# Instance normalisation on one core: the last tile stored in two pieces, and the final waits in the order of the stores

## The chip, the cores and the metric

The kernel runs on one core of a Trainium2 chip. The metric is the device time of one execution in microseconds (us). A profile shows the span from the first to the last instruction, some 1.7 us less than the device time. Even so, about one run in five of these kernels lies 1.5 to 7 us above the rest, so I quote medians, and for differences of a microsecond I read the profiles, where one event can be measured from another.

## The reference

```python
def setup_inputs():
    x = np.random.randn(8, 64, 32, 64, 64).astype(np.float32)   # 268 MB
    eps = np.float32(1e-5)

def reference(x, eps):
    mean = np.mean(x, axis=(2, 3, 4), keepdims=True)
    var = np.var(x, axis=(2, 3, 4), keepdims=True)
    return ((x - mean) / np.sqrt(var + eps)).astype(np.float32)
```

Each of the 512 instances (batch times channel) has 131072 elements. All of x is read once and written once.

## The kernel before

A tile has 128 rows (partitions) of 12288 floats: 6 MiB, three chunks of 4096 columns. There are 42 tiles in four buffers ("slots"), after two small parts of 2 MiB each. SyncE issues the loads, ScalarE the stores. VectorE and ScalarE share the work on a tile: sums, squares, and at the end the scaling, in place. VectorE scales chunks 0 and 1, ScalarE scales chunk 2, and then ScalarE issues the store:

```python
    # VectorE, end of a tile
        eng.reciprocal(out=a[:, SCALES : SCALES + 3], ...)._wait_ge(rooted[lane], c1)...
        eng.tensor_mul(out=a[:, SHIFTS : SHIFTS + 3], ...)...then_inc(shifted[lane], 1)
        eng.tensor_scalar(out=chunk[0], ...)._wait_ge(scaled[lane], c1).then_inc(done[lane], 1)
        eng.tensor_scalar(out=chunk[1], ...)._wait_ge(shifted[lane], c1).then_inc(done[lane], 1)

    # ScalarE, end of a tile
        eng.activation(out=chunk[2], ...)._wait_ge(shifted[lane], c1).then_inc(done[lane], 1)
        eng.dma_start(out=dst, in_=t)._wait_ge(done[lane], c3).then_inc(stored[lane], 16)

    # SyncE: loads
        ...
            eng.dma_start(out=slots[s][:], in_=x_t[it * SLOTS + s])._wait_ge(
                stored[s], c16).then_inc(landed[s], 16)
        ...
        for s in range(SLOTS):                       # the final waits
            eng.wait_ge(stored[s], 16 * len(range(s, n_tiles, SLOTS)))
```

The last tile is number 41, in slot 1, so its wait is the second of the four.

Of the kernel before, what the change touches and what calls it, by code (L numbers as in the profile page):

```python
# [9 lines left out]
def kernel(  # L10
# [20 lines left out]
    CHUNK = 4096  # L31
    THIRDS = 3
    COLS = THIRDS * CHUNK
    SLOTS = 4
    PART = P * CHUNK // n_elem

    n_tiles = n_inst // PART // THIRDS
# [7 lines left out]
    def tiles_of(ap):  # L45
        first = n_parts * P * CHUNK
        return ap[first : first + n_tiles * P * COLS].rearrange(
            "(k p f) -> k p f", p=P, f=COLS
        )

    def part_of(ap, m):
        return ap[m * P * CHUNK : (m + 1) * P * CHUNK].rearrange("(p f) -> p f", p=P)

    x_t, out_t = tiles_of(x_f), tiles_of(out_f)
# [24 lines left out]
    def semaphores(name, n=LANES):  # L79
        return [ctx.enter_context(nc.semaphore(f"{name}{i}")) for i in range(n)]  # L80
# [11 lines left out]
    done = semaphores("done")  # L92
    stored = semaphores("stored")
# [15 lines left out]
    def column(a, first, j):  # L109
        return a[:, first + j : first + j + 1]  # L110
# [95 lines left out]
            op1=Alu.add,  # L206
        )._wait_ge(shifted[lane], c1).then_inc(done[lane], 1)

    def tile_on_scalar(eng, t, lane, c1, c3, c4, c16, dst):
        a = small[lane]  # L210
        chunk = [t[:, i * CHUNK : (i + 1) * CHUNK] for i in range(THIRDS)]
        for j, part in ((1, chunk[1]), (2, chunk[2][:, : CHUNK - TURN])):
            eng.activation(  # L213
                out=unused[j - 1][:, : part.shape[1]],
                in_=part,
                func=Act.Identity,
                accum_out=column(a, SUMS, j),
            )._wait_ge(landed[lane], c16).then_inc(summed[lane], 1)
        for j in (1, 2):
            eng.activation(  # L220
                out=unused[j - 1][:],
                in_=chunk[j],
                func=Act.Square,
                bias=column(a, MEANS, j),
                accum_out=column(a, SQUARES, j),
            )._wait_ge(centred[lane], c1).then_inc(squared[lane], 1)
        eng.activation(  # L227
            out=a[:, ROOTS : ROOTS + 3],
            in_=a[:, VARS : VARS + 3],
            func=Act.Sqrt,  # L230
            bias=eps_t[:, 0:1],
        )._wait_ge(gathered[lane], c1).then_inc(rooted[lane], 1)
        eng.activation(  # L233
            out=chunk[2],
            in_=chunk[2],
            func=Act.Identity,
            scale=column(a, SCALES, 2),
            bias=column(a, SHIFTS, 2),
        )._wait_ge(shifted[lane], c1).then_inc(done[lane], 1)
        eng.dma_start(out=dst, in_=t)._wait_ge(done[lane], c3).then_inc(  # L240
            stored[lane], 16
        )

# [80 lines left out]
    def over_tiles(eng, on_part, on_tile, with_target=False):  # L324
        for m, (lane, t) in enumerate(parts):
            more = (part_of(out_f, m),) if with_target else ()
            on_part(eng, t, lane, *more)
        counts = [
            ctx.enter_context(eng.register(f"{on_tile.__name__}_c{m}"))
            for m in (1, 3, 4, 16)  # L330
        ]
        for c, m in zip(counts, (1, 3, 4, 16)):
            eng.reg_mov(c, m)
        with eng.Fori(0, ROUNDS) as it:
            for s in range(SLOTS):
                more = (out_t[it * SLOTS + s],) if with_target else ()
                on_tile(eng, slots[s][:], s, *counts, *more)
            for c, m in zip(counts, (1, 3, 4, 16)):
                eng.reg_add(c, c, m)
        for k in range(ROUNDS * SLOTS, n_tiles):  # L340
            c = k // SLOTS + 1
            more = (out_t[k],) if with_target else ()
            on_tile(eng, slots[k % SLOTS][:], k % SLOTS, c, 3 * c, 4 * c, 16 * c, *more)

    def load_all(eng):
        for m, (lane, t) in enumerate(parts):
            eng.dma_start(out=t, in_=part_of(x_f, m)).then_inc(landed[lane], 16)
        for s in range(SLOTS):
            load = eng.dma_start(out=slots[s][:], in_=x_t[s])
            if s >= SLOTS - n_parts:  # L350
                load._wait_ge(stored[s + n_parts], 16)
            load.then_inc(landed[s], 16)
        c16 = ctx.enter_context(eng.register("load_c16"))
        eng.reg_mov(c16, 16)
        with eng.Fori(1, ROUNDS) as it:  # L355
            for s in range(SLOTS):
                eng.dma_start(out=slots[s][:], in_=x_t[it * SLOTS + s])._wait_ge(  # L357
                    stored[s], c16
                ).then_inc(landed[s], 16)
            eng.reg_add(c16, c16, 16)  # L360
        for k in range(ROUNDS * SLOTS, n_tiles):
            eng.dma_start(out=slots[k % SLOTS][:], in_=x_t[k])._wait_ge(
                stored[k % SLOTS], 16 * (k // SLOTS)
            ).then_inc(landed[k % SLOTS], 16)

        for s in range(SLOTS):
            eng.wait_ge(stored[s], 16 * len(range(s, n_tiles, SLOTS)))

    def set_up(eng):
        count = 0  # L370
# [55 lines left out]
        return count  # L426

    load_all(nc.sync)
    set_by = set_up(nc.gpsimd)
    nc.vector.wait_ge(ready, set_by)  # L430
    over_tiles(nc.vector, part_on_vector, tile_on_vector)
    nc.tensor.wait_ge(ready, set_by)
    over_tiles(nc.tensor, part_on_tensor, tile_on_tensor)
    nc.scalar.preload_act_table(Act.Sqrt)
    nc.scalar.wait_ge(ready, set_by)
    over_tiles(nc.scalar, part_on_scalar, tile_on_scalar, with_target=True)


# [33 lines left out]
```

## Time and profile before

| | before |
|---|---|
| median of the first three runs | 1247.06 us (1246.88 to 1249.86) |
| span in the profile | 1245.2 us, granted clock 1.000 |
| moved | 536.89 MB, 431 GB/s over the span |
| busy: VectorE, ScalarE, DMA | 65%, 61%, 99.7% |

The page's row of tenths shows who is busy when; here the DMA row is full. For a change at the end of the kernel only the end counts, and there the average says nothing. 16 DMA engines share each store, 8 rows of the tile each, one packet per row, and each engine adds a small packet for the semaphore when its rows are through (the store queue's 6336 packets are 128 + 16 for each of its 44 stores).

### The profile page before, as it was taken

The page shows a single profiled execution, that of the slowest core. Times are in us where ns is not written, and L with a number is a line of the kernel's source. Part 1 is how long each engine was busy: PE and PEld are TensorE (multiplying, and loading weights), DVE is VectorE, ACT ScalarE, POOL GpSimd, SP SyncE. Part 2 cuts the span into 40 slices and gives each one's busy share as a digit, 9 for nine tenths or more (in the row PEclk, how much of TensorE's full clock was granted, in tenths as well). Part 3 has the DMA queues.
Part 4 walks back from the last instruction along what each step waited for, and adds up shares of the span by engine and source line. Part 5 has one row for each costly group of instructions (what it writes and reads, how often), then busy time and mean ns, then how long its engine had stood idle before and what let it go on. Part 6 is the DMA issues. An engine that isn't in the chain of part 4 may idle for free.

```text
span 1245.2 us, 1950 instructions
## 1 busy us (share of the span) xinstructions
PE 52.7 (4%) x176; PEld 44.1 (4%) x176; DVE 811.6 (65%) x724; ACT 757.7 (61%) x433; POOL 2.7 (0%) x15
## 2 busy tenths in 40 slices
PE   0000000000000000000000000000000000000000
PEld 0000000000000000000000000000000000000000
DVE  2887666666666666666666666666666666666663
ACT  5876555566666665665556665666566555566653
POOL 0000000000000000000000000000000000000000
DMA  9999999999999999999999999999999999999998
GB/s 396 429 430 434 444 433 429 431 429 441 439 433 431 429 429 444 436 429 433 431 433 442 434 431 431 429 434 444 433 431 431 429 442 437 431 433 429 429 444 368
DMA packets 12674, 536.89 MB, mean 431 GB/s; under 512 B 1408, under 2 KB 1408, under 8 KB 1408
## 3 DMA queue, kind: packets, MB, share of 16 engines
q1 hardware_dynamic: 6336, 268.44, 49.9%
q10 hardware_dynamic: 6336, 268.44, 49.8%
q14 instruction: 2, 0.02, 0.0%
HBM read 268.44 MB, written 268.44 MB: 431 GB/s over the span
## 4 chain that ended last, share of the span: by engine, by line
another core or an unknown queue 82%; DMA 9%; DVE 3%; ACT 2%; SPq 1%; issue 1%; PE 0%; ACTq 0%
DMA slot<-in_x_dram 6%; DMA out_dram<-slot 4%; ACT unused L220 2%; SPq L357 1%; DVE small L157 1%; DVE slot L200 1%; DVE slot L193 1%; ACT unused L213 0%; PE psum L250 0%; DVE small L137 0%; DVE small L125 0%; DVE small L131 0%; DVE small L143 0%; SPq L355 0%
## 5 line engine op out<-in xcount | busy, mean ns | idle before, releaser
L213 ACT ACTIVATE unused<-slot 128x4096 uint8<-128x4096 f32 x84 | 249.3, 2968 | 310.5 <-DMA slot<-in_x_dram 308.1
L157 DVE TENSOR_REDUCE small<-slot 128x1 f32<-128x4096 f32 x84 | 255.3, 3081 | 279.6 <-DMA slot<-in_x_dram 279.6
L220 ACT ACTIVATE unused<-slot,small 128x4096 uint8<-128x4096 f32 x84 | 310.8, 3701 | 65.3 <-DVE small L143 65.3
L171 DVE CUSTOM_DVE_ANT_0 unused<-slot 128x4096 uint8<-128x4096 f32 x42 | 185.9, 4426 | 1.4
L233 ACT ACTIVATE slot<-slot,small 128x4096 f32<-128x4096 f32 x42 | 159.7, 3802 | 18.5 <-DVE small L188 18.5
L200 DVE TENSOR_SCALAR slot<-slot,small 128x4096 f32<-128x4096 f32 x42 | 101.1, 2408 | 0.0
L164 DVE TENSOR_SCALAR slot<-slot,small 128x4096 f32<-128x4096 f32 x42 | 98.8, 2353 | 1.5
L250 PE MATMUL psum<-small,avg 128*128 128x12 f32 (+1 forms) x168 | 50.4, 375 | 1144.3 <-DVE small L125 1144.3
L193 DVE TENSOR_SCALAR slot<-slot,small 128x4096 f32<-128x4096 f32 x42 | 98.6, 2347 | 0.0
L250 PEld LDWEIGHTS psum<-small,avg 128*128 128x128 f32 x168 | 42.1, 311 | 1152.5 <-DVE small L125 1152.5
L131 DVE TENSOR_REDUCE small<-psum 128x3 f32<-128x12 f32 x84 | 14.2, 169 | 58.0 <-PE psum L250 58.0
L227 ACT ACTIVATE small<-small,eps_t 128x3 f32<-128x3 f32 x42 | 12.6, 299 | 62.6 <-DVE small L143 62.6
L125 DVE TENSOR_TENSOR small<-small,belongs 128x12 f32<-128x12 f32 x84 | 14.3, 170 | 31.9 <-ACT unused L220 29.5
L185 DVE RECIPROCAL small<-small 128x3 f32<-128x3 f32 x42 | 7.4, 176 | 15.4 <-ACT small L227 15.4
L137 DVE TENSOR_TENSOR small<-small,belongs 128x9 f32<-128x9 f32 x84 | 14.3, 170 | 2.9
L220 ACT ACTIVATION_READ_ACCUMULATOR unused<-slot,small 128x1 f32 x84 | 15.7, 186 | 0.0
L213 ACT ACTIVATION_READ_ACCUMULATOR unused<-slot 128x1 f32 x84 | 15.6, 186 | 0.0
L143 DVE TENSOR_REDUCE small<-small 128x3 f32<-128x9 f32 x84 | 13.6, 162 | 2.9
L263 DVE TENSOR_REDUCE small<-slot 128x1 f32<-128x2048 f32 x2 | 4.6, 2282 | 8.9 <-DMA slot<-in_x_dram 8.9
L289 ACT ACTIVATE unused<-slot,small 128x4096 uint8<-128x4096 f32 x2 | 7.4, 3707 | 2.0 <-DVE small L266 2.0
L286 ACT ACTIVATE unused<-slot 128x2048 uint8<-128x2048 f32 x2 | 3.8, 1910 | 7.1 <-DMA slot<-in_x_dram 6.6
L188 DVE TENSOR_TENSOR small<-small 128x3 f32<-128x3 f32 x42 | 6.8, 162 | 1.4
(26 smaller groups left out, 21.1 us busy)
## 6 DMA issues: line engine op xcount, KB each, us to landing
slot<-in_x_dram SPq DMA_DIRECT2D x42, 6144.0 KB, 39.9
out_dram<-slot ACTq DMA_DIRECT2D x42, 6144.0 KB, 54.2
slot<-in_x_dram SPq DMA_DIRECT2D x2, 2048.0 KB, 10.0
out_dram<-slot ACTq DMA_DIRECT2D x2, 2048.0 KB, 27.7
```

What stands on the lines that cost most here:

```text
L125: eng.tensor_tensor(out=block(a, by_both, n, m), in0=spread(a, at, m), in1=belongs[:, :, :m], op=Alu.mult,)._wait_ge(*wait).then_inc(steps ...
L131: eng.tensor_reduce(out=a[:, by_instance : by_instance + n], in_=p.rearrange("p (n m) -> p n m", m=m), axis=AXIS, op=Alu.add,)._wait_ge(st ...
L137: eng.tensor_tensor(out=block(a, by_chunk, n, n), in0=spread(a, by_instance, n), in1=belongs[:, :, :n].rearrange("p i c -> p c i"), op=Alu ...
L157: eng.reduce_sum(out=column(a, SUMS, j), in_=part, axis=AXIS)._wait_ge(landed[lane], c16).then_inc(summed[lane], 1)
L164: eng.tensor_scalar(out=chunk[0], in0=chunk[0], scalar1=column(a, MEANS, 0), scalar2=None, op0=Alu.add,)._wait_ge(centred[lane], c1).then_ ...
L171: eng.tensor_tensor_reduce(out=unused[2][:], in0=chunk[0], in1=chunk[0], scale=1.0, scalar=0.0, op0=Alu.mult, op1=Alu.add, accum_out=colum ...
L193: eng.tensor_scalar(out=chunk[0], in0=chunk[0], scalar1=column(a, SCALES, 0), scalar2=None, op0=Alu.mult,)._wait_ge(scaled[lane], c1).then ...
L200: eng.tensor_scalar(out=chunk[1], in0=chunk[1], scalar1=column(a, SCALES, 1), scalar2=column(a, SHIFTS, 1), op0=Alu.mult, op1=Alu.add,)._w ...
L213: eng.activation(out=unused[j - 1][:, : part.shape[1]], in_=part, func=Act.Identity, accum_out=column(a, SUMS, j),)._wait_ge(landed[lane], ...
L220: eng.activation(out=unused[j - 1][:], in_=chunk[j], func=Act.Square, bias=column(a, MEANS, j), accum_out=column(a, SQUARES, j),)._wait_ge ...
L233: eng.activation(out=chunk[2], in_=chunk[2], func=Act.Identity, scale=column(a, SCALES, 2), bias=column(a, SHIFTS, 2),)._wait_ge(shifted[l ...
L250: eng.matmul(out=p[:, col : col + THIRDS * m], lhsT=avg[PART][:], rhs=a[:, at + m : at + m + THIRDS * m], start=True, stop=True,)._wait_ge ...
```

## The change

The intent: in front of the last store the DMA engines seem to stand still for 2 us. If chunk 0 goes out as soon as it is scaled, the gap is filled. The other part puts the wait for the last tile behind the three others; its target is 16 higher, since the last tile now has two stores.

```diff
-    def tile_on_scalar(eng, t, lane, c1, c3, c4, c16, dst):
+    def tile_on_scalar(eng, t, lane, c1, c3, c4, c16, dst, last=False):
 ...
+        at = 0
+        if last:
+            at = CHUNK
+            eng.dma_start(out=dst[:, :at], in_=chunk[0])._wait_ge(
+                done[lane], c3 - 2
+            ).then_inc(stored[lane], 16)
         eng.activation(out=chunk[2], ...)._wait_ge(shifted[lane], c1).then_inc(done[lane], 1)
-        eng.dma_start(out=dst, in_=t)._wait_ge(done[lane], c3).then_inc(
+        eng.dma_start(out=dst[:, at:], in_=t[:, at:])._wait_ge(done[lane], c3).then_inc(
             stored[lane], 16
         )
 ...
-        for s in range(SLOTS):
-            eng.wait_ge(stored[s], 16 * len(range(s, n_tiles, SLOTS)))
+        for k in range(n_tiles - SLOTS, n_tiles):
+            uses = k // SLOTS + 1 + (k == n_tiles - 1)
+            eng.wait_ge(stored[k % SLOTS], 16 * uses)
```

(The caller passes `last` for tile 41 alone.) ScalarE's stream now has the wait for chunk 0 ahead of its own scaling of chunk 2.

## The prediction

> **What bounds the kernel now.** I read three things in this order: the DMA row and the queues of the page, the stretches of the whole span, and then the last 25 us in ever narrower stretches, because the change touches nothing earlier than the last tile.
>
> The page, DMA row of the 40 slices and the queues:
>
> ```profile
> DMA  9999999999999999999999999999999999999998
> ...
> q1 hardware_dynamic: 6336, 268.44, 49.9%
> q10 hardware_dynamic: 6336, 268.44, 49.8%
> ```
>
> The row stands at 9 from the first slice to the last but one. Loads (q1) and stores (q10) together take 99.7% of the 16 DMA engines' time, while VectorE has 65% and ScalarE 61%. The kernel is bound by its DMA engines. The stretches view with the first and last tiles cut off says how tightly (columns: stretch, its length, busy time of PE, PEld, DVE, ACT and POOL, clock, DMA share, GB/s):
>
> ```profile
> 55.00:1215.00 1160.00, 48.56 (x162) 40.61 (x162) 770.99 (x687) 710.39 (x405) 0.00 (x0) 1.00 1.00 434
> ```
>
> So only the two ends of the kernel can hold anything to gain. A store of a tile is 128 rows of 49152 bytes, which are 8 packets on each of the 16 engines; in the packet records one such packet takes 1.815 us (median of all), so one engine moves 27.1 GB/s. All 536.87 MB at 16 times that is 1239.1 us, of the 1245.2 us of the span: 6.1 us are not transfer.
>
> The end, as the timeline has it:
>
> ```profile
> 1222.87 0.16 DVE L188 TENSOR_TENSOR small<-small 128x3 f32<-128x3 f32 x1
> 1222.95 2.35 DVE L193 TENSOR_SCALAR slot<-slot,small 128x4096 f32<-128x4096 f32 x1
> 1223.07 3.80 ACT L233 ACTIVATE slot<-slot,small 128x4096 f32<-128x4096 f32 x1 [0.44 <-DVE small L188]
> 1225.21 2.41 DVE L200 TENSOR_SCALAR slot<-slot,small 128x4096 f32<-128x4096 f32 x1
> 1227.65 0.35 ACTq L240 DMA_DIRECT2D out_dram<-slot  x1
> ```
>
> VectorE scales chunk 0 (to 1225.30) and chunk 1 (to 1227.62); ScalarE scales chunk 2 beside it (to 1226.87); then the store is issued. The view of that issuing line says when it lands: 16.2 us later, at 1243.9.
>
> ```profile
> DMA to landing us min/median/max: 16.2/16.2/16.2
> ```
>
> What do the DMA engines do meanwhile? Stretches of the end; packets count where they start, so a share over 1.00 is a batch that starts together:
>
> ```profile
> 1222.00:1226.45 4.45, 0.00 (x0) 0.00 (x0) 4.02 (x6) 3.68 (x2) 0.00 (x0) 1.00 0.84 364
> 1226.46:1228.45 1.99, 0.00 (x0) 0.00 (x0) 1.16 (x1) 0.41 (x1) 0.00 (x0) 1.00 0.12 49
> 1228.45:1228.93 0.48, 0.00 (x0) 0.00 (x0) 0.00 (x0) 0.00 (x0) 0.00 (x0) 1.00 3.62 1536
> 1228.93:1230.30 1.37, 0.00 (x0) 0.00 (x0) 0.00 (x0) 0.00 (x0) 0.00 (x0) 1.00 0.08 36
> 1230.30:1241.20 10.90, 0.00 (x0) 0.00 (x0) 0.00 (x0) 0.00 (x0) 0.00 (x0) 1.00 1.00 433
> ...
> 1241.60:1243.00 1.40, 0.00 (x0) 0.00 (x0) 0.00 (x0) 0.00 (x0) 0.00 (x0) 1.00 0.08 35
> ```
>
> There is a hole in front of the last store, from 1226.46 to 1228.45. It is what the change means to fill. But it isn't a hole in all engines. The DMA view of 1226.46 to 1228.45 and that of 1228.93 to 1230.3:
>
> ```profile
> DMA packets 14, 0.10 MB, mean 49 GB/s; under 512 B 12, under 2 KB 12, under 8 KB 12
> ...
> DMA packets 1, 0.05 MB, mean 36 GB/s; under 512 B 0, under 2 KB 0, under 8 KB 0
> ```
>
> In the hole two whole rows start: 12 of the 14 packets are the small ones that count the semaphore. They are the last rows of the store before, on two engines that lag the other 14 by about one row. In the packet records their rows end at 1228.70 and 1228.93, when the new store has been in the queue for half a microsecond; 14 engines start its first row at 1228.51 to 1228.66, the last engine at 1228.934, the instant it is done with the old one. That engine (packets bear no engine here; I match each to the one that ended when it starts) then takes eight rows without a pause and ends at 1243.43, when the other 15 had ended at 1243.08 to 1243.24. **The engine that ends last had no hole.** The lag isn't a chance of this moment: between the first and the last of the 16 counts of a transfer lie 0.6 us at the first tile, 2.0 us a quarter of the way in and 2.2 to 2.6 us from the middle to the end, so it builds up and stays.
>
> **What the Trainium skill says.** "DMA: Bandwidth & Descriptors", section "Why a DMA increments its semaphore by 16 and not by 1": the engines of one transfer finish independently, and only the full count tells that all has landed. The trace agrees: of the store before the last, 14 counts came between 1226.79 and 1227.91, the two others at 1229.03 and 1229.42. The same page, "Anatomy of one DMA": waits are on the issuing sequencer, not in the DMA engines. It agrees too: the issue starts 0.03 us after VectorE ended; so a wait put in ScalarE's stream holds ScalarE. The same page, "Latency and other measured facts", has some 600 ns to the first byte for this kind of queue; here the first row starts 0.85 us after the issue starts and 0.50 us after it ends, and I use 0.85.
>
> **The change part by part.**
>
> First piece. ScalarE now waits for chunk 0 before it scales chunk 2. Chunk 0 is done at 1225.30 as before, the issue takes 0.35 us (1225.33 to 1225.68) and its rows can start at 1225.33 + 0.85 = 1226.18. The first engine is free at 1226.45, so 14 engines go straight on (from 1226.45 to 1227.56) and the two laggards at 1228.70 and 1228.93, as before. The hole closes: 14 engines gain between 1.0 and 2.1 us.
>
> ScalarE's part moves back. Chunk 2 starts at about 1225.73 in place of 1223.07, 2.66 us later, takes 3.80 us, and ends at 1229.53, after VectorE's chunk 1 (1227.62), so it now sets the second issue: 1229.55, 1.90 us later than the whole store was issued before. Its rows can start at 1229.55 + 0.85 = 1230.40.
>
> Is that late? Rows of 16384 bytes took 0.611 us (median of the early, small stores), so eight take 4.89 us. The earliest engine is through with the first piece at 1226.45 + 4.89 = 1231.34, 0.94 us after the second piece is there. ScalarE's delay is hidden.
>
> The last engine. Before: eight rows at 1.815 us, 14.52 us. From 0.611 us for 16384 bytes and 1.815 us for 49152, a row costs 0.009 us and 0.602 us per 16384 bytes, so one of 32768 is worth 1.213 us (an estimate). After: 8 x (0.611 + 1.213) = 14.59 us, and one semaphore packet more, 0.009 us: 0.08 us longer from the same start, 1228.93. It ends at about 1243.5. The other laggard ends at 1228.70 + 14.60 = 1243.3, the 14 at 1241.1 to 1242.2: they idle at the end in place of at the beginning.
>
> Final waits. Before, the last tile's wait comes second of four, and two that are long satisfied follow it; after, it is last. In the trace, the wait that ends with the landing ends at 1243.92, and one more waiting instruction lies at 1243.965 to 1244.00; the reordering is worth some 0.04 us.
>
> The sum: +0.08 - 0.04 = +0.04 us at the end, and nothing elsewhere, since loops and buffers are untouched. That is nothing.
>
> **The rivals.** (1) *The hole was on the path.* If all engines were alike, the store would end sooner by the 14 engines' gain, at most 1228.51 - 1226.45 = 2.06 us, and the slowest of them 1.0; 1245.0 to 1246.1 us. For it: the aggregate hole of 2 us is real, and the lag may be smaller in runs without a profile. (2) *The laggards speed up when the others are done*, because memory is less busy. Then part of the 1 to 2 us comes back. Against it: a laggard's row from 1226.88 to 1228.70 ran while 13 to 14 engines were idle and took 1.815 us, like all others. (3) *The later second piece takes the place of the hole*: if ScalarE or its issue took over 0.94 us longer than I reckon, the 14 engines would have a new gap; it would have to exceed some 2 us before they, and not the laggards, set the end. Time then 1247 to 1248. (4) *Short rows, 48 KiB apart, are slower in HBM* than rows that follow each other: 10% of 4.9 us would be 0.5 us. Nothing in this trace shows such rows.
>
> **Range and chances.** The base is 1247.06 us, the median of three (1246.88, 1247.06, 1249.86). With my sum it stays; rival 1, to which I give one in four, and rival 2, one in ten, draw it down by some 1.2 us, so I take off 0.3: 1246.8 us. Spread of runs (two within 0.2 us, the third 2.9 us above) is larger than any of these effects. Range 1245.3 to 1248.4. Two per cent are 25 us; the whole last store takes 16.2 us, so neither side can be reached by this change; 0.5% each for surprises.
>
> **What would show it right or wrong.** Right: two issues at about 1225.3 and 1229.55; ScalarE's last scaling starting near 1225.7; no hole in the DMA share at 1226.5 to 1228.5; in the last 2 us of transfer only one or two engines still busy; the landing at 1243.9 to 1244.0 and the span within 0.3 us. Wrong: a landing 1 us or more earlier (rival 1 or 2; the lag of the last engine tells which: gone, or rows shorter than 1.8 us per 48 KiB), a second hole at 1231 to 1232 (rival 3), or rows of the first piece over 0.65 us (rival 4).

## The result

| | before | changed |
|---|---|---|
| median, 6 runs of each | 1248.31 us (1246.72 to 1252.91) | 1247.05 us (1246.87 to 1247.35) |
| span in the profile | 1245.2 us | 1245.6 us |
| packets of the store queue | 6336 | 6480 |

The ratio is 0.9986, with a 95% interval from 0.9968 to 1.0004: the same. A ratio is the mean time of one kernel's runs over that of the other's of the same rounds, so not quite the ratio of the medians. It is the three high runs of before that pull it below 1; the lowest runs of the two are 0.15 us apart, the changed kernel's the higher.

The end of the changed kernel, as the timeline has it (start, length, engine, line, operation):

```profile
1223.32 2.35 DVE L193 TENSOR_SCALAR slot<-slot,small 128x4096 f32<-128x4096 f32 x1
1225.58 2.41 DVE L200 TENSOR_SCALAR slot<-slot,small 128x4096 f32<-128x4096 f32 x1
1225.70 0.35 ACTq L237 DMA_DIRECT2D out_dram<-slot  x1
1226.09 3.80 ACT L240 ACTIVATE slot<-slot,small 128x4096 f32<-128x4096 f32 x1 [3.10 <-DVE slot L193]
1229.92 0.34 ACTq L247 DMA_DIRECT2D out_dram<-slot  x1
```

Everything in this run is 0.37 us later than in the run before the change, because the last load landed that much later (1206.11 and 1205.74). Apart from that it is as reckoned: ScalarE stands idle for 3.10 us until VectorE has scaled chunk 0, issues the first piece, scales chunk 2, and issues the rest.

The stretches of the changed kernel (length, busy time of the five engines, clock, DMA share, GB/s; packets count where they start), and the packets of the first of them:

```profile
1226.53:1228.11 1.58, 0.00 (x0) 0.00 (x0) 1.46 (x1) 1.58 (x1) 0.00 (x0) 1.00 0.93 394
...
1231.49:1240.61 9.12, 0.00 (x0) 0.00 (x0) 0.00 (x0) 0.00 (x0) 0.00 (x0) 1.00 1.06 458
1240.61:1241.20 0.59, 0.00 (x0) 0.00 (x0) 0.00 (x0) 0.00 (x0) 0.00 (x0) 1.00 0.13 56
1241.42:1242.64 1.22, 0.00 (x0) 0.00 (x0) 0.00 (x0) 0.00 (x0) 0.00 (x0) 1.00 0.25 107
1242.64:1243.80 1.16, 0.00 (x0) 0.00 (x0) 0.00 (x0) 0.00 (x0) 0.00 (x0) 1.00 0.07 28
```

```profile
DMA packets 50, 0.62 MB, mean 394 GB/s; under 512 B 14, under 2 KB 14, under 8 KB 14
```

The hole is gone: where before the DMA share was 0.12 for 2 us, it is 0.93, and 36 rows start in 1.58 us. But the idle time has only moved. In the last 3 us the share falls to 0.25 and then 0.07, which is one engine of 16. In the packet records the engines end like this (the small packet for the semaphore included; a packet bears no engine number, so each is matched to the one that ended when it starts):

| | first 12 engines | next three | last engine |
|---|---|---|---|
| before | 1243.08 to 1243.20 | 1243.20 to 1243.24 | 1243.44 |
| changed | 1241.22 to 1241.83 | 1242.64 to 1242.84 | 1243.87 |

And the landings (the time from the start of an issue until the last of its 16 counts is in), from the views of the issuing lines: of tile 40's store, the first piece and the second piece.

```profile
DMA to landing us min/median/max: 30.9/30.9/30.9
...
DMA to landing us min/median/max: 9.0/9.0/9.0
...
DMA to landing us min/median/max: 14.4/14.4/14.4
```

So the last piece lands at 1229.92 + 14.4 = 1244.3, against 1243.9 before. Fifteen engines are done earlier, twelve of them by 1.4 to 1.9 us, and the kernel isn't.

### The profile page after: what moved, and what is told of

The parts are those of the page before. It is cut to its first block, busy times and chain, and to the rows that moved or that the text cites. A ratio compares the mean times of both kernels' runs of the same rounds, so it can differ in the third digit from the quotient of the medians.

```text
span 1245.6 us, 1951 instructions
## 1 busy us (share of the span) xinstructions
PE 52.6 (4%) x176; PEld 44.0 (4%) x176; DVE 811.4 (65%) x724; ACT 757.7 (61%) x433; POOL 2.7 (0%) x15
## 3 DMA queue, kind: packets, MB, share of 16 engines
q1 hardware_dynamic: 6336, 268.44, 49.9%
q10 hardware_dynamic: 6480, 268.44, 49.8%
## 4 chain that ended last, share of the span: by engine, by line
another core or an unknown queue 82%; DMA 9%; ACT 3%; DVE 2%; SPq 1%; issue 1%; PE 0%; ACTq 0%
DMA slot<-in_x_dram 6%; DMA out_dram<-slot 4%; ACT unused L221 2%; SPq L364 1%; DVE small L157 1%; DVE slot L193 1%; ACT unused L214 0%; DVE slot L200 0%; ACT slot L240 0%; PE psum L257 0%; DVE small L137 0%; DVE small L125 0%; DVE small L131 0%; DVE small L143 0%
## 6 DMA issues: line engine op xcount, KB each, us to landing
out_dram<-slot ACTq DMA_DIRECT2D x1, 4096.0 KB, 14.4
```

## The experiments

**Theory A:** the time is that of the DMA engine that lags, and this engine never had the hole: it was still writing the store before when the hole was open. **Theory B:** the hole was on the path and some of its gain was real, but was given back, by ScalarE's late start, by the second transfer or by the shorter rows. A minor question is whether the high runs of before have to do with the order of the waits.

Where two kernels or more were run together they ran on the same chip and share the runs of the kernel before.

### The changed kernel again

No edit.

> The changed kernel once more, beside the kernel before, for the spread of both. Theory A (the DMA engine that ends last never had the hole, so closing the hole is worth nothing): median 1246.9 to 1247.4, ratio to before 1.000 within 0.0005 among the runs without an outlier; in the profile the last engine again takes its rows of the last tile without a pause and is busy 1 us or more after most of the others. Theory B (the hole was on the path, and half of the gain shows): 0.999 or less, with the lowest runs 1 us below the lowest of before. Also open: the kernel before had three of six runs 2.7 to 6 us above its lowest, this one none; if that belongs to the kernels and not to chance, it comes again.

Measured: 1247.08 us median (1246.95 to 1253.76, 6 runs); before 1246.96 (1246.56 to 1252.16, 11 runs); ratio 1.0005, interval 0.9984 to 1.0026. In the profile 13 engines end at 1241.06 to 1241.67, two at 1242.59 and 1242.76, one at 1243.65. As theory A has it. The changed kernel has a high run too, 1253.76, so the high runs don't belong to the kernel before.

### The waits alone

```diff
-        for s in range(SLOTS):
-            eng.wait_ge(stored[s], 16 * len(range(s, n_tiles, SLOTS)))
+        for k in range(n_tiles - SLOTS, n_tiles):
+            eng.wait_ge(stored[k % SLOTS], 16 * (k // SLOTS + 1))
```

> The kernel before with only the final waits in the order of the stores; the last tile is stored whole. Theory A: no effect over 0.1 us on the span; the stretch from the last landing to the end of the span stays 1.28 to 1.31 us (1.28 before, 1.31 after the change). The step of the prediction (0.04 us gained) would make it 1.24. A theory that the order of the waits is what removes the slow runs of before expects no run here over 1248.5.

Measured: 1246.92 us (1246.70 to 1247.12, 6 runs), ratio 0.9993 (0.9979 to 1.0007), span 1245.2. From the last landing to the end of the span are 1.30 us, against 1.28 before: no gain. The trace shows why. The compiled program has its own order: in the changed kernel the wait for the last tile shares one instruction with that for tile 39 (it ends at 1244.386), and the wait for tile 38 still comes after it, on a branch at 1244.432. None of the six runs was high, but the next two kernels, which have this order of waits, have one each, so nothing follows from that.

### The first piece from another queue

The first piece is issued by SyncE; chunk 0's scaling counts a semaphore of its own (`early`), and ScalarE waits for nothing but the shift:

```diff
+        # SyncE, ahead of the final waits
+        eng.dma_start(out=out_t[k][:, :CHUNK], in_=slots[k % SLOTS][:, :CHUNK])._wait_ge(
+            early, 1).then_inc(stored[k % SLOTS], 16)
-        # ScalarE
-            eng.dma_start(out=dst[:, :at], in_=chunk[0])._wait_ge(done[lane], c3 - 2)...
```

> The first piece is issued from SyncE, which is idle then, and ScalarE no longer waits for VectorE before it scales chunk 2. So ScalarE ends 2.7 us sooner than in the changed kernel, and the second piece is issued 1.9 us sooner, when VectorE ends chunk 1. Theory A: nothing gained, landing and span as in the changed kernel within 0.5 us (the lag of the last engine differs from run to run by that), 1247.1. The rival that the gain of the hole was real and was given back by ScalarE's late start: 1 us or more faster, 1246.0 or less.

The timeline of this kernel:

```profile
1223.07 3.80 ACT L236 ACTIVATE slot<-slot,small 128x4096 f32<-128x4096 f32 x1 [0.44 <-DVE small L189]
1225.22 2.40 DVE L201 TENSOR_SCALAR slot<-slot,small 128x4096 f32<-128x4096 f32 x1
1225.33 0.34 SPq L374 DMA_DIRECT2D out_dram<-slot  x1
1227.65 0.35 ACTq L243 DMA_DIRECT2D out_dram<-slot  x1
```

Both pieces are in their queues as early as they can be, the second 1.9 us sooner than in the changed kernel, counted from the start of chunk 0's scaling (4.70 and 6.60 us). Measured: 1247.01 us (1246.81 to 1249.36), ratio 0.9997 (0.9982 to 1.0013), span 1245.3, last landing 1243.97. ScalarE's late start cost nothing; that form of theory B falls.

### The first piece late

```diff
-                done[lane], c3 - 2
+                done[lane], c3 - 1
```

> The changed kernel with the first piece held until VectorE has scaled chunk 1 too: both pieces later by 2.3 us (first issue as late as the whole store before, second issue 4.2 us after it). The hole of about 2 us is back in the engines that do not lag. Theory A: still 1247.1 and a landing within 0.5 us of the changed kernel's, because the last engine is free only 0.4 to 0.8 us after the first rows can start. Theory B, the hole on the path: 1 to 2 us slower than the changed kernel.

The stretches of this kernel and the landing of its second piece, which was issued at 1232.03:

```profile
1226.46:1228.65 2.19, 0.00 (x0) 0.00 (x0) 1.31 (x1) 0.45 (x1) 0.00 (x0) 1.00 0.11 45
1228.66:1230.00 1.34, 0.00 (x0) 0.00 (x0) 0.00 (x0) 1.34 (x1) 0.00 (x0) 1.00 1.31 550
```

```profile
DMA to landing us min/median/max: 12.1/12.1/12.1
```

The hole is back in full, 2.19 us at a share of 0.11, and the second piece is issued 2.3 us later than in the changed kernel, counted in the same way. It lands at 1244.1 all the same, and the median is 1246.90 us (1246.72 to 1250.36), ratio 0.9998 (0.9982 to 1.0015). With the hole the engines end together, 15 of them at 1243.33 to 1243.47 and one at 1243.64; without it they end apart, the last at the same time. This is the plainest evidence against theory B: the hole can be opened and closed and the time doesn't follow.

### The hole put on the path

If theory A holds, the same split has to pay as soon as all engines are idle and even when the last store comes. In both kernels VectorE waits, in the last tile only, until tile 40's store has landed:

```diff
+        if last:
+            k = n_tiles - 2
+            eng.wait_ge(stored[k % SLOTS], 16 * (k // SLOTS + 1))
         eng.reciprocal(out=a[:, SCALES : SCALES + 3], ...
```

> The kernel before, but VectorE waits, in the last tile alone and ahead of the reciprocal, until the store of the tile before has landed in full. So all 16 DMA engines are idle and even when the last store comes. About 6.8 us later than in the kernel before (landing of that store at 1229.4 in place of the reciprocal at 1222.66): scaling ends near 1234.4, first rows near 1235.3, landing near 1250.1, time near 1253.3. The engines should end within 0.2 us of each other.

> The same pause in the changed kernel. Theory A says that the split is worth nothing in the real kernel only because one engine is still behind; with all engines idle the first rows start 2.3 us sooner (VectorE's time for one chunk), the second piece is there 0.6 us before the first is through, and 0.07 us go to the shorter rows: 2.25 us less than the paused kernel with a whole store, in the span and in the time, near 1251.1. A theory that splitting a store cannot gain on this chip (cost of a second transfer, shorter rows at a pitch of 48 KiB, ScalarE held up) makes it 0 to 1 us less.

Issue and landing of the store in the paused kernel with a whole store:

```profile
1234.25 0.35 ACTq L243 DMA_DIRECT2D out_dram<-slot  x1
...
DMA to landing us min/median/max: 15.9/15.9/15.9
```

The two issues in the paused kernel with the split store, and the landing of the second piece:

```profile
1232.03 0.35 ACTq L240 DMA_DIRECT2D out_dram<-slot  x1
...
1236.26 0.34 ACTq L250 DMA_DIRECT2D out_dram<-slot  x1
...
DMA to landing us min/median/max: 11.8/11.8/11.8
```

Measured: 1253.31 us (1253.17 to 1254.20, 5 runs) whole, 1251.13 us (1251.07 to 1254.31, 5 runs) split: 2.18 us between the medians. Counted from the start of chunk 0's scaling, the whole store lands after 20.64 us (1229.55 to 1250.19) and the split one after 18.40 us (1229.65 to 1248.05): 2.24 us less, and 2.25 were expected. In both, all 16 engines end within 0.17 us of each other. Two of the five split runs are high (1254.07 and 1254.31), so the ratios to the kernel before (1.0054 whole, 1.0047 split, intervals 1.0040 to 1.0068 and 1.0033 to 1.0060) don't tell the two apart; the lowest runs do (1253.17 and 1251.07), and the two traces. So the split works, and its whole worth was there to be had; in the kernel as it is, the lag of one engine takes it away. A second transfer and shorter rows cost nothing that shows.

### Looking for a kernel that beats both

If the lagging engine had less to write at the end, the gain could be had. The Trainium skill, "DMA: Bandwidth & Descriptors", section "Why a DMA increments its semaphore by 16 and not by 1", says that a transfer runs on the largest number of engines up to 16 that divides its rows, the lowest-numbered ones. So 120 rows go to 15 engines and 8 rows to 8, and a transfer can leave out the highest-numbered. Three kernels, each the changed one with the second piece in more transfers (cut to the slices; the final wait counts the added transfers too):

```diff
 # uneven: the last 2048 columns apart
+  (slice(0, P), slice(at, COLS - 2048)), (slice(0, 120), slice(COLS - 2048, COLS)), (slice(120, P), slice(COLS - 2048, COLS))
 # short_tail: the same columns apart, all 128 rows in one transfer
+  (at, COLS - 2048), (COLS - 2048, COLS)
 # uneven_rows: the second piece by rows
+  for rows in (slice(0, 120), slice(120, P)):
```

> Looks for the engine that lags. The changed kernel, but the last 2048 columns of the last tile are stored in two transfers of their own: rows 0 to 119, which by the Trainium skill go to 15 engines (the last one left out), and rows 120 to 127, which go to the first 8, one row each. If the engine that ends last is the one left out, it has 2.5 us less to move, the others at most 0.3 us more, and the landing comes 0.8 to 1.1 us sooner than in the changed kernel: 1246.1. If it is one of the first 8, the landing is 0.3 us later, if one of the other seven the same: 1247.1 to 1247.4. In each case the profile shows how many engines take 8, 9 or none of the short rows.

Measured: 1247.86 us (1247.20 to 1248.81, 5 runs); before 1246.82 beside it; ratio 1.0010 (0.9997 to 1.0024). None of the three cases expected: the landing is later than in any of them. The skill's counts hold: the semaphore got 57 updates in place of 64, one of them before any row had landed, which is what 16 + 16 + (1 + 15) + (1 + 8) makes. But many short rows were slow: 47 of 128 took over 0.33 us, up to 1.23, with a median of 0.309. The last landing came 15.63 us after that of tile 40's store, 1.1 us more than in the changed kernel. Short rows or their placing? The next two tell.

> Why did the uneven kernel end 0.6 us later than the changed one: its short rows (8192 bytes at a pitch of 49152), or their placing on 15 and 8 engines? Here the same 2048 last columns are one more transfer of all 128 rows, so 8 short rows to each of 16 engines. If short rows are slow in themselves, many take more than the 0.309 us that is their median and the landing comes 0.5 us or more after the changed kernel's, time 1247.6 or more. If it is the placing, all short rows take 0.31 us, the landing is within 0.5 us of the changed kernel's (0.15 us more for 8 more packets and a count), time 1247.1 to 1247.3.

Measured: 1247.37 us (1246.85 to 1252.57, 6 runs), ratio 1.0009 (0.9993 to 1.0025). All short rows took 0.309 to 0.328 us, and the last landing came 14.58 us after that of tile 40's store, against 14.52 in the changed kernel. So rows of 8192 bytes aren't slow in themselves; what slows them goes with the split into 120 and 8 rows.

> The changed kernel with the second piece in two transfers by rows: rows 0 to 119 on 15 engines, 8 rows of 32768 bytes each; rows 120 to 127 on the first 8 engines, one row each. If the engine that ends last is the one left out, it is done near 1234 and the rest end at 1242.4 to 1244.0, so the landing is the same to 1 us sooner, 1246.2 to 1247.2. If it is one of the first 8, it takes a ninth row and the landing is 1.2 us later, 1248.3; if one of the other seven, 1247.1. If the placing on 15 engines slows rows down, many of these take well over 1.22 us.

Measured: 1256.93 us (1256.73 to 1257.14, 5 runs), ratio 1.0075 (1.0062 to 1.0088), 10 us slower. The stretches of this kernel from the start of its second piece:

```profile
1231.30:1236.00 4.70, 0.00 (x0) 0.00 (x0) 0.00 (x0) 0.00 (x0) 0.00 (x0) 1.00 1.14 307
1236.00:1241.00 5.00, 0.00 (x0) 0.00 (x0) 0.00 (x0) 0.00 (x0) 0.00 (x0) 1.00 0.81 197
```

The engines are busy (0.81) and move less than half as much (197 GB/s) as in the same place of the changed kernel (458). Rows of 32768 bytes take 2.16 us in the mean, against 1.21 (both transfers taken together). None of my three cases foresaw 10 us; the clause on placing did in kind. Which engine lags isn't settled, but it isn't the one left out here: in the packet records that one ends its first piece at 1232.03 and gets nothing more, while the one that lags ends its first piece at 1233.73 and goes straight on with a row of the second. Why the placing is slow stays open. The skill's section "The descriptor swizzle" on the same page says that in a transfer of 128 partitions each engine keeps to one port of the SBUF; that 120 rows break this would fit, but it is a guess: no run here shows ports.

No kernel was found that beats both.

## Why the prediction was right

The forecast was 1246.8 us, with 1245.3 to 1248.4; the medians were 1247.05 and 1247.08. The number alone proves little: the range also holds most of what rival 1 would have given (1245.0 to 1246.1). Nor is the 1.26 us between the medians of the result a gain: three high runs of before make it, and its medians beside the experiments were 1246.82 to 1246.96. The base, the median of three runs, had some luck: one of the three was high, and with two it would have been off by some 2 us. And one chance in four and one in ten, 35% in all, of 1.2 us are 0.42 and not the 0.3 that was taken off; the sum by itself, without this, would have been nearer (1247.1). What speaks for the prediction are the landings and packets. Of its signs, the landing (1243.9 to 1244.0) and the span (within 0.3 us) are missed as they stand, with 1244.34 and 0.47 more; without the 0.37 us by which the last load was late they are 1243.97 and 0.10. Point by point:

- **The bound.** The DMA engines, and at the end the one that lags: shown; why it lags stays open. The table gives, from the semaphore records, the last landing of tile 40's store and of the last tile. Whatever is done to the hole, the difference is that of eight rows on one engine.

| kernel | tile 40 | last | difference |
|---|---|---|---|
| before | 1229.42 | 1243.90 | 14.48 |
| waits alone | 1229.39 | 1243.86 | 14.47 |
| changed | 1229.82 | 1244.34 | 14.52 |
| changed, again | 1229.58 | 1244.13 | 14.55 |
| first piece late | 1229.57 | 1244.11 | 14.54 |
| short tail | 1230.06 | 1244.64 | 14.58 |

  The differences between the spans (1245.2 to 1246.0) are mostly in the first column, which holds the lag and how late the last load was, and both change from run to run. From SyncE's queue it is 13.94, because on the last engine a row of the first piece is then written between tile 40's last row and its count (1228.94 to 1229.55), so that tile 40 lands later (1230.03); the last landing, 1243.97, is none the later for it. The margin was small: in the kernel before, the other 15 engines ended only 0.19 us ahead of the last (1243.24 and 1243.43), with a lag of 2.63 us. From these figures I estimate that with a lag under some 2.4 us a part of the gain would have been real.
- **The first piece** was to be issued at 1225.33 and the hole to close: 1225.70, which is 1225.33 on the clock of the run before; closed.
- **ScalarE's delay** of 2.66 us hidden: shown by the kernel that removes it and gains nothing. The margin was reckoned at 0.94 us; the first engine was through with the first piece at 1231.50, and its rows of the second could have started 0.85 us after the issue, at 1230.77: 0.73 us.
- **The shorter rows**: reckoned at 0.08 us more on the last engine, measured 0.05. Its rows took 14.50 us before (1228.93 to 1243.43) and 14.55 after (1229.31 to 1243.86).
- **The waits**: reckoned at 0.04 us gained. Wrong in a small way: nothing, since the compiled program doesn't keep the order of the source.
- **The two laggards**: there were two in the trace of before, four in that of the changed kernel (three by 1.5 to 1.7 us, one by 2.9), so that four engines, and not "one or two", were busy in the last 2 us, until 1242.64. How many lag differs; that the last engine lags the first by 2.4 to 3.2 us at tile 40 was so in all 11 profiles.
- **The rivals.** The first (all engines alike) got one chance in four; the paused pair shows that its mechanism is sound, with 2.2 us, and that only its premise is false here. The second (laggards speed up alone) falls: the last row of the changed kernel took 1.213 us like the others of its size, though for all but its first 0.2 us no other engine was at work. (The row that the prediction used against it, from 1226.88, had 13 to 14 engines idle only from 1227.4 on.) The third and fourth didn't come about with 16 engines: in the changed kernel no engine waited between the pieces (0.73 us of margin), and no row of the first piece took over 0.642 us.

## What to carry to other kernels

A DMA share of 0.12 isn't an empty machine: it may be two engines of 16 at work, and if one of those ends last, the hole of the others costs nothing. Before filling a gap, ask which single resource ends last and whether that one was idle in the gap; a count of packets in a narrow stretch answers it. And to tell "worthless" from "worthless here", put the gap on the path on purpose, with a pause, and see whether the trick pays then.

## What the Trainium skill lacked or had wrong

- "DMA: Bandwidth & Descriptors": how far the engines drift apart under a steady load isn't there. The section "Latency and other measured facts" has engines 7 and 15 as usually slower and gives, as a guess, a cause that only the other kind of queue has. Here, with the queues of SyncE and ScalarE alone, the first and the last of a transfer's 16 counts were 0.4 to 1.3 us apart at the first tile and 2.4 to 3.2 us at tile 40, so that guess doesn't cover this case. Which engine it was the runs don't tell, except that in one it wasn't the one left out.
- The same page, "Specifications", has some 27 GiB/s for an engine; a row of 49152 bytes in 1.815 us is 27.1 GB/s, or 25.2 GiB/s. Its fabric ceiling of 435 GB/s fits the 433 to 434 measured.
- The same page tells how many engines a transfer gets, but not what fewer than 16 do to a row: with the second piece split into 120 rows on 15 engines and 8 rows on 8, a row of 32768 bytes took 2.16 us in the mean against 1.21, and the kernel 10 us more.
- The same page has some 600 ns to the first byte on this kind of queue; from the start of the issue to the first row were 0.85 us, and from the end of the last row to its count 0.47 us.
- I found no page that says that the order of waits in the source isn't kept in the compiled program: the last tile's wait, last in the source, was followed by that of tile 38 (1244.386 and 1244.432 us).
